# An RWKV-7 recurrence step in another order: masks split by operand, the inverse's last rows ahead of the second state, two stores issued by SP

## The chip, the cores and the metric

One core of a Trainium2 chip runs the whole program. The metric is the device time of one execution in microseconds, the median of several runs. TensorE (PE) multiplies matrices, VectorE (DVE), ScalarE (ACT) and GpSimd (POOL) work elementwise, SyncE (SP) issues DMAs; ACT can issue DMAs too.

## The reference

A decoder trunk of two layers over 1024 tokens of width 1024, with RMS norms and residual adds. The even layer (a chunked gMLP beside dilated attention) is not touched. The odd layer is RWKV-7 time mixing: projections r, k, v, a gate, a data-dependent decay, and a recurrence over time for each of 16 heads with a 64 x 64 state:

```
sa    = state @ (-kk_t)
state = state * w_t + outer(sa, kk_t * a_t) + outer(v_t, k_t)
y_t   = state @ r_t
...
y = (groupnorm(y) + bonus) * silu(g) ;  x = x + y @ w_o
```

## The kernel before

All arithmetic is in float32; a projection's operands are split into a high and a low float32r part and multiplied in three passes (`mm3`).

**The recurrence in chunks.** Time is cut into 16 chunks of 64 tokens. In a chunk the recurrence is a triangular system: U = X (W), where X is the inverse of a 64 x 64 triangular matrix per head that does not depend on the state, and W comes from the state and the chunk's keys. For chunk c, with the names of the text below:

- `al` (`alphas`): scores that give the triangular matrix M and the masked operand AK. `sM` (`store_M`) writes M to DRAM in four DMAs for a pair of chunks, `lM` (`load_M`) reads it back in another layout as Nt.
- `ip`, `ia`, `ie`, `ib`, `ic` (`inverse_p` to `inverse_c`): the inverse of a pair of chunks. POOL clears its tiles (`ip`); DVE builds diagonal blocks of 8 (`ia`, `ie`) and then block rows, eight pieces in all, of which `ibN` does the next N; `ic` stores the result to DRAM. `lX` (`load_X`) reads it back as X, and `mx`, `ma`, `mb` merge its halves of 32 with two small sets of matmuls and ACT copies between them.
- `sc` (`scores`): the scores of the outputs, copied to MY. `msk` (`masks`): POOL zeroes the upper triangles of MY and AK, two instructions for each and chunk.
- `dec` (`decayed`): POOL scales BK by the chunk's decay; `T` (`transposed`): PE transposes the scaled BK, ACT copies it to BKT.
- `U`: PE multiplies X with W (and begins the next chunk's W with AK and V), ACT copies U into UV in two halves. `st` (`state`): PE multiplies BKT with UV, DVE adds the product to the next state S. `keep`: POOL scales S by the decay ahead of that add. `W`: PE multiplies S (and the previous chunk's outputs with S). `Y` (`Yout`): PE multiplies MY with UV; `Yd` (`store_Y`): two DMAs store the outputs of a pair of chunks.
- `ld`, `uv`: SP loads A, BK and v of a later chunk. `g`: one eighth of a gate projection tile (three matmuls of 512 columns), which fills PE; every eighth such piece ends with a copy and a store issued by ACT. `gl`, `gx`: load and split of that gate's weights.

**One step** is a pair of chunks c = 2b and c + 1; in it the recurrence runs for this pair, the inverse of the next pair is finished (`ib2` and the later `ib`, `ic0`, `lX0`, merge) and the inverse of the pair after is begun (`lM0`, `ia0`, `ie0`, `ib3`). There are six steps (b = 0 to 5) between an opening part (`SCAN_START`) and a closing part (`SCAN_END`) in which the layer's output stage begins: the last pair of chunks, the output norm and the projection.

**What sets the order.** PE, DVE, ACT, POOL and SP each execute their instructions strictly in the order in which the strings `SCAN_START`, `SCAN_STEP` and `SCAN_END` name them (a manual schedule), each engine as soon as its next instruction's inputs and buffers are there. SP and ACT each have a DMA queue. A DMA also waits for the landing of the DMA that used its completion semaphore before; eight semaphores go round. The text of a step:

```
    "U0 al0 ib2 st0 al1 sM0 uv0 Y0 keep1 ib1 W1 sc0 ib1 U1 uv1 ld6 st1 sc1 ib1 ic0 dec0 Y1 lM0 W2 keep2 ip0 lX0 "
    "gx1 sc2 Yd0 T0 msk0 g2 ia0 sc3 g2 mx0 ma0 ie0 g2 dec1 T1 mb0 msk1 g3 ib3 ld7 gl2")
```

A number is an argument: for most names the chunk or pair counted from the step's own (`ops`), for `sc` half chunks, for `g` and `ib` the number of pieces. The two state adds of a step are those of `st0` and `st1`.

Of the kernel before, what the change touches and what calls it, by code (L numbers as in the profile page):

```python
# [12 lines left out]
OP = mybir.AluOpType  # L13
# [5 lines left out]
KT = D // P  # L19
# [6 lines left out]
CH = 64  # L26
# [24 lines left out]
    "q0 k0 h0 z2 h1 q1 h2 k1 h3 va0 s0 h4 u0 h5 z3 h6 z0 h7 va1 s1 u1 z1")  # L51
SCAN_START = (
# [4 lines left out]
SCAN_STEP = (  # L57
    "U0 al0 ib2 st0 al1 sM0 uv0 Y0 keep1 ib1 W1 sc0 ib1 U1 uv1 ld6 st1 sc1 ib1 ic0 dec0 Y1 lM0 W2 keep2 ip0 lX0 "
    "gx1 sc2 Yd0 T0 msk0 g2 ia0 sc3 g2 mx0 ma0 ie0 g2 dec1 T1 mb0 msk1 g3 ib3 ld7 gl2")
SCAN_END = (  # L60
# [6 lines left out]


def order(text):
    for tok in text.split():  # L70
        name = tok.rstrip("0123456789")
        yield name, int(tok[len(name):])
# [905 lines left out]
class Rwkv:  # L978
# [71 lines left out]
    def store_M(self, b2):  # L1050

        M = self.ring("M", b2, 2, None)
        for k in range(4):
            b = k % 2
            self.g.nc.scalar.dma_start(self.g.MA_d[b2][k].rearrange("c q t s -> t (c q) s"),
                                     M[32 * k:32 * k + 32, :, :, 32 * b:32 * b + 32].rearrange("p c q s -> p (c q) s"))

    def decayed(self, c):
# [13 lines left out]
                    nc.tensor.transpose(pt[:, i, :], BK[:, 4 * q + i].rearrange("p j t -> p (j t)"), g.ident)  # L1072
                nc.scalar.activation(BKT[:, 4 * q:4 * q + 4], pt, AF.Copy)

    def masks(self, c):
        nc, t = self.g.nc, self.T[c]
        for r in (slice(0, 64), slice(64, 128)):
            nc.gpsimd.affine_select(t["MY"][r], t["MY"][r], pattern=[[0, NHD], [1, CH]], compare_op=OP.is_ge, fill=0.0,
                                    base=0, channel_multiplier=-1)
            nc.gpsimd.affine_select(t["AK"][r], t["AK"][r], pattern=[[0, KT], [1, CH]], compare_op=OP.is_ge, fill=0.0,  # L1080
                                    base=-1, channel_multiplier=-1)

# [210 lines left out]

    def store_Y(self, b):
        for e in range(2):
            self.g.nc.scalar.dma_start(self.g.Y_d[b].rearrange("(c t) h d -> t c h d", c=2)[:, :, 8 * e:8 * e + 8],
                                     self.Y[64 - 64 * e:128 - 64 * e])

    def start(self, gate):
        g, nc = self.g, self.g.nc

        def zs(i):
            nc.gpsimd.memset(self.new_S(0), 0.0)

        self.pm = g.bB([P, 2, 2, 4, CH], "pm")
        ops = dict(L=gate.load, wx=gate.split, xl=gate.load_x, ld=self.load,
                   g=lambda i: [next(gate.rest, None) for _ in range(i)],
                   sc=lambda i: self.scores(i // 2, i % 2), al=self.alphas, sM=self.store_M, lM=self.load_M,  # L1310
                   ip=self.inverse_p, ia=self.inverse_a, ie=self.inverse_d, ib=lambda i: [next(self.rows, None) for _ in range(i)],
                   ic=self.inverse_c, lX=self.load_X, mx=self.merge_x, ma=self.merge_a, mb=self.merge_b,
                   dec=self.decayed, T=self.transposed, msk=self.masks,
                   uv=self.load_uv, V=lambda i: list(self.Wkeys(i)), W=self.W, keep=self.keep, zs=zs)
        for name, i in order(SCAN_START):
            ops[name](i)

    def ops(self, b, gate):
        c = 2 * b
        return dict(  # L1320
            U=lambda i: self.U(c + i), st=lambda i: self.state(c + i), keep=lambda i: self.keep(c + i),
            W=lambda i: self.W(c + i), sc=lambda i: self.scores(c + 4 + i // 2, i % 2),
            al=lambda i: self.alphas(c + 4 + i), sM=lambda i: self.store_M(b + 2 + i),
            lM=lambda i: self.load_M(b + 2 + i), ip=lambda i: self.inverse_p(b + 2 + i),
            ia=lambda i: self.inverse_a(b + 2 + i),
            ie=lambda i: self.inverse_d(b + 2 + i), ib=lambda i: [next(self.rows, None) for _ in range(i)],
            ic=lambda i: self.inverse_c(b + 1 + i), lX=lambda i: self.load_X(b + 1 + i),
            mx=lambda i: self.merge_x(b + 1 + i), ma=lambda i: self.merge_a(b + 1 + i),
            mb=lambda i: self.merge_b(b + 1 + i), dec=lambda i: self.decayed(c + 4 + i),
            T=lambda i: self.transposed(c + 4 + i), Y=lambda i: self.Yout(c + i),  # L1330
            msk=lambda i: self.masks(c + 4 + i), R=lambda i: list(self.Ystate(c + i)),
            uv=lambda i: self.load_uv(c + 2 + i), ld=lambda i: c + i < NC and self.load(c + i),
            g=lambda i: [next(gate.rest, None) for _ in range(i)],
            gl=lambda i: b + KT + i < 2 * KT and gate.load(b + KT + i),
            gx=lambda i: b + KT + i < 2 * KT and gate.split(b + KT + i),
            Yd=lambda i: self.store_Y(b + i))
# [10 lines left out]
    def end(self, gate, o):  # L1347

        g = self.g
        ops = self.ops(NB - 2, gate)  # L1350

        def store_Y(i):
            self.store_Y(NB - 2 + i)
            if i == 0:
                self.new_Y()

        self.new_Y()
        ops.update(Yd=store_Y, S=lambda i: o.setup_norm() if i else o.setup(), Sb=lambda i: o.bonus(), Lr=o.load, Ls=o.split, Fl=o.operands, Fm=o.centre, Fv=o.variance, Fy=o.scaled,
                   Ft=o.gated, Fs=o.parts, Pl=o.residual, p=o.project, Pn=o.norm, Po=o.store)
        for name, i in order(SCAN_END):  # L1360
            ops[name](i)
# [199 lines left out]
```

## Time and profile before

| | us |
|---|---|
| median of 3 runs | 1486.93 (1485.79 to 1487.78) |
| profiled execution, its own time | 1486.46 |
| its span in the trace | 1484.4 |
| PE busy | 1305.9 (88% of the span) |
| DVE busy | 913.4 (62%) |
| ACT busy | 628.8 (42%) |
| POOL busy | 544.7 (37%) |

The trace holds one execution, instruction by instruction, with times from the span's start. The busy shares are averages over the whole program; the recurrence's six steps lie between about 1080 and 1303 us, the closing part behind them.

### The profile page before, as it was taken

The page shows a single profiled execution, that of the slowest core. Times are in us where ns is not written, and L with a number is a line of the kernel's source. Part 1 is how long each engine was busy: PE and PEld are TensorE (multiplying, and loading weights), DVE is VectorE, ACT ScalarE, POOL GpSimd, SP SyncE. Part 2 cuts the span into 40 slices and gives each one's busy share as a digit, 9 for nine tenths or more (in the row PEclk, how much of TensorE's full clock was granted, in tenths as well). Part 3 has the DMA queues.
Part 4 walks back from the last instruction along what each step waited for, and adds up shares of the span by engine and source line. Part 5 has one row for each costly group of instructions (what it writes and reads, how often), then busy time and mean ns, then how long its engine had stood idle before and what let it go on. Part 6 is the DMA issues. An engine that isn't in the chain of part 4 may idle for free.

```text
span 1484.4 us, 30909 instructions
## 1 busy us (share of the span) xinstructions
PE 1305.9 (88%) x12773; PEld 1110.6 (75%) x12773; DVE 913.4 (62%) x1489; ACT 628.8 (42%) x1188; POOL 544.7 (37%) x353
## 2 busy tenths in 40 slices
PE   5899999799998999999998869998977878687877
PEld 5887788788896799978854537896766667567877
DVE  8741536663556436760698997332676776668884
ACT  4421535543554324652555554232434444354322
POOL 8750102030213512221343353023744444367751
PEclk9999999899999999999999989998988998889999
DMA  6277446240543435133187547427675565675412
GB/s 220 86 265 188 114 128 171 72 128 15 148 108 115 141 106 152 47 110 108 50 243 196 132 118 196 105 74 218 167 234 157 154 156 145 160 220 212 145 34 95
DMA packets 253276, 209.16 MB, mean 141 GB/s; under 512 B 79648, under 2 KB 215424, under 8 KB 253136
## 3 DMA queue, kind: packets, MB, share of 16 engines
q1 hardware_dynamic: 230336, 191.98, 44.4%
q10 hardware_dynamic: 22800, 15.21, 3.7%
q8 instruction: 100, 1.64, 0.5%
q14 instruction: 40, 0.33, 0.1%
HBM read 135.71 MB, written 71.43 MB: 140 GB/s over the span
## 4 chain that ended last, share of the span: by engine, by line
PE 51%; DVE 17%; DMA 12%; ACT 7%; issue 6%; POOL 4%; SPq 2%; ACTq 1%; DVEq 0%; POOLq 0%
PE pj L153 33%; PE pj L943 3%; PE pt L572 2%; PE pj L1473 2%; PE pj L711 2%; DMA X<-XT 1%; DMA XT<-xm 1%; DMA w<-in_rw_a_dram 1%; DMA BK<-BK_d 1%; PE ch L1271 1%; PE op L580 1%; ACT wh L105 1%; PE sp L559 1%; PE sp L562 1%; ACT UV L1250 1%
## 5 line engine op out<-in xcount | busy, mean ns | idle before, releaser
L106 POOL TENSOR_TENSOR wl<-wraw,wh 128x1024 fp32r<-128x1024 f32 x38 | 95.6, 2518 | 174.2 <-ACT wh L105 161.5
L153 PE MATMUL pj<-hh,wh 128*128 128x512 f32 x320 | 127.3, 398 | 0.0
L153 PE MATMUL pj<-hh,wl 128*128 128x512 f32 x320 | 126.7, 396 | 0.0
L153 PE MATMUL pj<-hl,wh 128*128 128x512 f32 x320 | 126.6, 396 | 0.0
L106 DVE TENSOR_TENSOR wl<-wraw,wh 128x1024 fp32r<-128x1024 f32 x46 | 71.7, 1564 | 84.7 <-ACT wh L105 44.0
L105 ACT ACTIVATE wh<-wraw 128x1024 fp32r<-128x1024 f32 x84 | 88.2, 1057 | 66.0 <-DMA wraw<-in_w_in_even_dram 23.3
L153 PE MATMUL pj<-xl,wh 128*128 128x512 f32 x256 | 104.2, 408 | 2.5 <-DVE xl L740 2.5
L153 PE MATMUL pj<-xh,wh 128*128 128x512 f32 x256 | 103.8, 408 | 2.5 <-ACT ks L789 2.5
L153 PE MATMUL pj<-xh,wl 128*128 128x512 f32 x256 | 103.6, 405 | 0.2 <-POOL wl L106 0.2
L566 DVE CUSTOM_DVE_ANT_0 sc<-sp,tb 128x128 f32<-128x128 f32 (+3 forms) x64 | 48.2, 754 | 58.0 <-PE sp L562 49.6
L1473 PE MATMUL pj<-wh,yl 128*128 128x256 f32 x256 | 74.1, 289 | 6.4 <-POOL yl L106 6.4
L1473 PE MATMUL pj<-wh,yh 128*128 128x256 f32 x256 | 74.8, 292 | 5.2 <-DVE x L1477 5.2
L153 PE MATMUL pj<-wh,hh 128*128 128x256 f32 x256 | 74.7, 295 | 2.9 <-ACT hh L265 2.6
L737 DVE SCALAR_TENSOR_TENSOR xm<-hT,pr,xm 128x512 f32<-128x512 f32 x56 | 49.0, 917 | 44.1 <-ACT xm L736 43.7
L153 PE MATMUL pj<-wh,hl 128*128 128x256 f32 x256 | 74.8, 293 | 1.2 <-DVE hl L266 1.2
L153 PE MATMUL pj<-wh,yl 128*128 128x256 f32 x256 | 73.8, 288 | 1.9 <-POOL yl L624 1.9
L153 PE MATMUL pj<-wl,hh 128*128 128x256 f32 x256 | 74.3, 291 | 0.0
L1473 PE MATMUL pj<-wl,yh 128*128 128x256 f32 x256 | 73.8, 288 | 0.0
L153 PE MATMUL pj<-wh,yh 128*128 128x256 f32 x256 | 73.3, 286 | 0.5 <-ACT yh L623 0.5
L153 PE MATMUL pj<-wl,yh 128*128 128x256 f32 x256 | 72.9, 285 | 0.0
L153 PE MATMUL pj<-wh,xh 128*128 128x256 f32 x256 | 72.2, 282 | 0.1
L153 PE MATMUL pj<-wl,xh 128*128 128x256 f32 x256 | 72.2, 282 | 0.0
(320 smaller groups left out, 4063.2 us busy)
## 6 DMA issues: line engine op xcount, KB each, us to landing
wraw<-in_w_in_even_dram SPq DMA_DIRECT2D x28, 512.0 KB
tb<-tb SPq DMA_DIRECT2D x16, 512.0 KB
A_d<-AR SPq DMA_DIRECT2D x16, 512.0 KB
wraw<-in_rw_wg_dram SPq DMA_DIRECT2D x16, 512.0 KB
A<-A_d SPq DMA_DIRECT2D x16, 512.0 KB
BK<-BK_d SPq DMA_DIRECT2D x16, 512.0 KB
xt<-in_x_dram SPq DMA_DIRECT2D x8, 512.0 KB
dv<-vt SPq DMA_DIRECT2D x16, 256.0 KB
```

The source lines that it names most:

```text
L105: nc.scalar.activation(hi, raw, AF.Copy)
L106: sub.tensor_tensor(lo, raw, hi.bitcast(F32), OP.subtract)
L153: nc.tensor.matmul(ps, a(k), b(k), start=(n == 0), stop=(n == 3 * KT - 1))
L559: nc.tensor.matmul(sp[:, c0:c1], qs[:, b * P:(b + 1) * P], kh[:, c0:c1], start=True, stop=False)
L562: nc.tensor.matmul(sp[:, c0:c1], qs[:, b * P:(b + 1) * P], kl[:, c0:c1], start=False, stop=True)
L566: nc.vector.tensor_tensor_reduce(sc[:, :n], sp[:, :n], tb[:, off:off + n], 1.0, BIG, OP.add, OP.min, mn)
L572: nc.tensor.transpose(pt[:, j - j0, :], sc[:, j * P:(j + 1) * P], g.ident)
L580: nc.tensor.matmul(op[:, s0:QW], vt[:, j, :], pth[j // 4][:, j % 4, s0:QW], start=(j == 0), stop=False)
L711: nc.tensor.matmul(ps, x[:, 2 * kk + i, :], y[:, i, o:o + 512], start=(n == 0), stop=(n == 47))
L737: nc.vector.scalar_tensor_tensor(t, hT[kk, f][:, j, 0:512], g.pr[:, i, k:k + 1], t, op0=OP.mult, op1=OP.add)
L943: nc.tensor.matmul(ps, u[:, k], v[:, k % 2], start=(k == 0 and i == 0), stop=(k == KT - 1 and i == 2))
L1473: nc.tensor.matmul(ps[:, i, :], u[:, k], v[:, k % 4], start=(k == 0 and j == 0), stop=(k == KT - 1 and j == 2))
```

## The change

`masks` becomes two functions: `mask_AK`, called in a step for the chunks whose scores were just made (c+4, c+5), ahead of the second `W`, and `mask_MY`, called a step later than before (c+2, c+3), ahead of the second state. Of the inverse's rows the last three pieces are done together ahead of the second `U` (DVE) where one of them stood behind the second state; `ic0` follows ahead of `st1`. Scores `sc1` and two gate pieces move up, `mb0` and `T1` change places. The stores of M and of the outputs are issued by SP in place of ACT: M behind the first load of v, ahead of `ld6`; the outputs behind `lX0`, ahead of `ld7`. The first load of v of a step moves to the end of the step before. The opening and the closing part follow; the closing part now holds two `mask_MY` (four POOL instructions) that a step held before.

```diff
 SCAN_START = (
-    "ld3 L6 g4 msk0 ia0 L5 g2 al2 wx5 g2 sc4 T1 ld4 g3 al3 sM1 ie0 sc5 dec2 g3 wx6 ib8 sc6 g2 sc7 dec3 uv1 T2 zs0 "
-    "g3 ic0 g4 wx7 msk1 ip1 lM1 lX0 keep0 g4 T3 g5 L8 mx0 xl0 V0 ma0 g2 wx8 xl1 ia1 msk2 g2 xl2 mb0 ie1 W0 ld5 "
-    "msk3 g2 xl3 ib3")
+    "ld3 L6 g4 mA0 mY0 ia0 L5 g2 al2 wx5 g2 sc4 T1 ld4 g3 al3 sM1 ie0 sc5 dec2 g3 wx6 ib8 sc6 g2 sc7 dec3 uv1 T2 "
+    "zs0 g3 ic0 g4 wx7 mA1 mY1 ip1 lM1 lX0 keep0 g4 T3 g5 L8 mx0 xl0 V0 uv2 ma0 g2 wx8 xl1 ia1 mA2 g2 xl2 mb0 ie1 "
+    "W0 ld5 mA3 g2 xl3 ib3")
 SCAN_STEP = (
-    "U0 al0 ib2 st0 al1 sM0 uv0 Y0 keep1 ib1 W1 sc0 ib1 U1 uv1 ld6 st1 sc1 ib1 ic0 dec0 Y1 lM0 W2 keep2 ip0 lX0 "
-    "gx1 sc2 Yd0 T0 msk0 g2 ia0 sc3 g2 mx0 ma0 ie0 g2 dec1 T1 mb0 msk1 g3 ib3 ld7 gl2")
+    "U0 al0 ib2 st0 al1 Y0 uv1 keep1 mA0 mA1 W1 sM0 sc0 ib3 ld6 U1 sc1 g1 mY0 mY1 ic0 st1 dec0 lM0 Y1 g1 W2 keep2 "
+    "ip0 lX0 gx1 uv2 sc2 Yd0 T0 g1 sc3 ia0 ld7 mx0 ma0 dec1 ie0 g2 mb0 g2 T1 g2 ib3 gl2")
 SCAN_END = (
-    "Lr1 S0 Fl0 uv0 U0 g1 Fm0 ib2 Lr5 Lr2 st0 Y0 keep1 g1 ib1 W1 Lr6 uv1 ib1 Lr7 Ls5 U1 ib1 ic0 Ls2 gx1 lX0 Ls7 "
-    "st1 Sb0 Y1 Ls1 Ls6 Fv0 W2 keep2 Fl1 mx0 g4 ma0 g2 mb0 Yd0 Lr0 g2 Pl1 U2 Fm1 Fy0 st2 Fv1 Lr4 Lr3 Fy1 Y2 W3 "
...
+    "Lr1 S0 Fl0 U0 ib2 g1 Fm0 Lr5 Lr2 st0 Y0 keep1 mY0 mY1 g1 W1 ib3 Lr6 uv1 Lr7 Ls5 U1 ic0 Ls2 gx1 lX0 Ls7 st1 "
+    "Sb0 Y1 Ls1 Ls6 Fv0 W2 keep2 Fl1 mx0 g4 ma0 g2 mb0 Yd0 Lr0 g2 Pl1 U2 Fm1 Fy0 st2 Fv1 Lr4 Lr3 Fy1 Y2 W3 Ls0 "
...
@@ -1052,7 +1052,7 @@
         M = self.ring("M", b2, 2, None)
         for k in range(4):
             b = k % 2
-            self.g.nc.scalar.dma_start(self.g.MA_d[b2][k].rearrange("c q t s -> t (c q) s"),
+            self.g.nc.sync.dma_start(self.g.MA_d[b2][k].rearrange("c q t s -> t (c q) s"),
                                      M[32 * k:32 * k + 32, :, :, 32 * b:32 * b + 32].rearrange("p c q s -> p (c q) s"))
...
-    def masks(self, c):
+    def mask_AK(self, c):
+        nc, t = self.g.nc, self.T[c]
+        for r in (slice(0, 64), slice(64, 128)):
+            nc.gpsimd.affine_select(t["AK"][r], t["AK"][r], pattern=[[0, KT], [1, CH]], compare_op=OP.is_ge, fill=0.0,
+                                    base=-1, channel_multiplier=-1)
+
+    def mask_MY(self, c):
         nc, t = self.g.nc, self.T[c]
         for r in (slice(0, 64), slice(64, 128)):
             nc.gpsimd.affine_select(t["MY"][r], t["MY"][r], pattern=[[0, NHD], [1, CH]], compare_op=OP.is_ge, fill=0.0,
                                     base=0, channel_multiplier=-1)
-            nc.gpsimd.affine_select(t["AK"][r], t["AK"][r], pattern=[[0, KT], [1, CH]], compare_op=OP.is_ge, fill=0.0,
-                                    base=-1, channel_multiplier=-1)
...
     def store_Y(self, b):
         for e in range(2):
-            self.g.nc.scalar.dma_start(self.g.Y_d[b].rearrange("(c t) h d -> t c h d", c=2)[:, :, 8 * e:8 * e + 8],
+            self.g.nc.sync.dma_start(self.g.Y_d[b].rearrange("(c t) h d -> t c h d", c=2)[:, :, 8 * e:8 * e + 8],
                                      self.Y[64 - 64 * e:128 - 64 * e])
...
-                   dec=self.decayed, T=self.transposed, msk=self.masks,
+                   dec=self.decayed, T=self.transposed, mA=self.mask_AK, mY=self.mask_MY,
...
-            msk=lambda i: self.masks(c + 4 + i), R=lambda i: list(self.Ystate(c + i)),
+            mA=lambda i: self.mask_AK(c + 4 + i), mY=lambda i: self.mask_MY(c + 2 + i), R=lambda i: list(self.Ystate(c + i)),
```

## Rows read from the trace of the kernel before

**Rows 1.** Busy us by engine, six steps; then granted clock, DMA share, GB/s.
```profile
1080.00:1303.00 223.00, 171.06 (x4859) 144.90 (x4858) 158.05 (x251) 88.61 (x155) 93.02 (x92) 0.88 0.63 169
```

**Rows 2.** Waits of PE, six steps: total us, times, longest.
```profile
PE pt L1193 <- DMA X<-XT: 16.3, 9, 3.1
PE ch L1271 <- ACT UV L1250: 8.4, 11, 1.2
```

**Rows 3.** Timeline, DVE: first adds of steps 1, 6, closing part.
```profile
1091.36 0.68 DVE L1273 TENSOR_TENSOR S<-ch,S 128x512 f32<-128x512 f32 x1
...
1267.49 0.68 DVE L1273 TENSOR_TENSOR S<-ch,S 128x512 f32<-128x512 f32 x1
...
1307.12 0.69 DVE L1273 TENSOR_TENSOR S<-ch,S 128x512 f32<-128x512 f32 x1 [3.53 <-PE ch L1271]
```

**Rows 4.** Timeline, DVE, fourth step: start, us, instruction, idle before.
```profile
1198.68 0.68 DVE L1273 TENSOR_TENSOR S<-ch,S 128x512 f32<-128x512 f32 x1
...
1205.01 0.69 DVE L1273 TENSOR_TENSOR S<-ch,S 128x512 f32<-128x512 f32 x1 [2.02 <-PE ch L1271]
1205.62 0.95 DVE L1158 TENSOR_TENSOR tm<-DN,R 128x768 f32<-128x768 f32 x1
1206.60 0.95 DVE L1160 TENSOR_REDUCE xm<-tm 128x96 f32<-128x768 f32 x1
...
1214.10 0.92 DVE L1117 TENSOR_TENSOR DN<-Nt,rn 128x256 f32<-128x256 f32 x1 [2.74 <-DMA Nt<-MA]
...
1232.13 0.68 DVE L1273 TENSOR_TENSOR S<-ch,S 128x512 f32<-128x512 f32 x1
```

**Rows 5.** Timeline, SP's DMA issues, fourth step.
```profile
1201.09 1.11 SPq L1003 DMA_DIRECT2D BK<-BK_d  x1
1207.59 1.27 SPq L1167 DMA_DIRECT2D XT<-xm  x2
```

**Rows 6.** Timeline, ACT and PE, fourth step.
```profile
1196.29 1.97 ACTq L1055 DMA_DIRECT2D MA<-M  x4
...
1203.74 1.15 PE L1271 MATMUL ch<-UV,BKT 128*64 128x64 f32 x32 [1.23 <-ACT UV L1250]
...
1217.46 0.31 PE L1193 MATMUL pt<-X,M 32*32 32x32 f32 x8 [1.67 <-DMA X<-XT]
...
1227.97 1.20 ACT L1250 ACTIVATE UV<-ch 64x512 f32<-64x512 f32 x2 [2.16 <-PE ch L1246]
```

**Rows 7.** Waits of DVE, six steps.
```profile
DVE S L1273 <- PE ch L1271: 22.6, 6, 6.3
```

**Rows 8.** Groups of POOL's instructions, six steps (busy us, mean ns).
```profile
L1078 POOL TENSOR_SCALAR_AFFINE_SELECT MY<-MY 64x1024 f32<-64x1024 f32 x25 | 29.0, 1158 | 2.1 <-ACT MY L1031 1.4
...
L1080 POOL TENSOR_SCALAR_AFFINE_SELECT AK<-AK 64x512 f32<-64x512 f32 x25 | 18.3, 730 | 0.0
```

**Rows 9.** One group of DVE's instructions by shape, six steps.
```profile
L1127 DVE TENSOR_TENSOR tm<-DN 128x36 f32<-128x36 f32 x6 | 6.8, 1137 | 0.2
```

**Rows 10.** Timeline, DVE, sixth step, where POOL was idle beside it.
```profile
1286.99 0.20 DVE L1127 TENSOR_TENSOR tm<-DN 128x36 f32<-128x36 f32 x1
```

**Rows 11.** Timeline, POOL, fourth step.
```profile
1199.51 1.74 POOL L1262 TENSOR_TENSOR S<-S,EC 128x512 f32<-128x512 f32 x1 [10.84 <-DVE S L1273]
...
1208.30 1.06 POOL L1262 TENSOR_TENSOR S<-S,EC 128x512 f32<-128x512 f32 x1
1211.97 0.55 POOL L1102 MEMSET xm<- 128x544 f32 x1 [2.61 <-DMA XT<-xm]
...
1216.72 1.91 POOL L1062 TENSOR_TENSOR BK<-BK,EC 128x1024 f32<-128x1024 f32 x1
```

**Rows 12.** Timeline, ACT, end of the sixth step.
```profile
1296.12 1.20 ACT L1196 ACTIVATE rt<-pt 32x512 f32<-32x512 f32 x2 [8.01 <-DMA BK<-Y]
```

**Rows 13.** Timeline, POOL and DVE, closing part.
```profile
1312.14 10.49 POOL L106 TENSOR_TENSOR wl<-wraw,wh 128x1024 fp32r<-128x1024 f32 x4 [2.44 <-ACT wh L105]
...
1315.21 2.88 DVE L106 TENSOR_TENSOR wl<-wraw,wh 128x1024 fp32r<-128x1024 f32 x1 [1.77 <-ACT wh L105]
```

8 rows, old and new, of the table SCAN_END are left out of this document.

## The prediction

> **What bounds the kernel now.** First the busy time of the stretch that the change touches: six recurrence steps, from 1080 to 1303 us, in which TensorE is busy for 171.06 of 223 us at a mean granted clock of 0.88 [rows 1]. So a sixth of the tensor work's time there is waiting, and TensorE is not at its limit. Then who it waits for: 16.3 us go to the merge's first matmul, which waits for the DMA that brings back the inverse X, and 8.4 us to the state's matmul, which waits for ScalarE's two copies of U [rows 2]. Third, the distance between steps. The clearest mark is DVE's first state add of a step (call its end E): the first of the six is at 1091.36 and the sixth at 1267.49, so five steps take 176.1 us, 35.2 each; the next one, in the closing part, follows 39.6 later [rows 3].
>
> Last, one step read in order of time, the fourth. E is 1199.36. DVE does four more pieces of the inverse, then idles 2.02 us for TensorE before the second state add at 1205.01; only then come the last two rows, which end at 1207.55 [rows 4]. At 1207.59 SP issues the store of the inverse, and behind it in the same queue the load of the next Nt [rows 5]. Nt has landed when DVE starts the next inverse at 1214.10, and from there DVE works without a pause up to the next first add at 1232.13 [rows 4], 33.4 us after the last. TensorE stands still for it. This is a closed loop: E, rows, store, Nt, next inverse, next E. A second loop runs through X: the merge starts at 1217.46, when X has landed, and U is copied out at 1227.97 [rows 6]. In the other steps the hole before the second add is larger (six holes, 22.6 us, at most 6.3 [rows 7]), and the second loop decides.
>
> **The change, part by part.**
>
> *The last rows before the second add.* Two instructions, 1.93 us from 1205.62 to 1207.55 [rows 4], move from behind the add into the hole before it. The smallest hole is 2.02 us, so the add hardly moves. The store of the inverse goes out as soon as the six pieces are done: 3.63 us for the first four (1199.36 to the hole's start at 1202.99) and 1.93 for the last two, E+5.6 instead of E+8.2 here, and up to 7 us earlier where the hole was long.
>
> *The masks split.* Eight instructions on POOL, four of 1.16 us (MY) and four of 0.73 us (AK) [rows 8], lie today beside DVE's next inverse. There DVE's small two-operand instructions are held up: the worst, of 36 elements, takes 1.14 us on average and 0.20 with POOL idle [rows 9, 10], a loss of 0.94. It is one of eight such forms; the other seven, compared in the same way, lose from 0 to 0.6 each and 2.6 together, so 3.5 of the chain's 18.0 us. Moved ahead, the masks lie beside the three two-operand pieces that follow E. Each of these can lose from nothing to the rest of one mask, 0.6 on average if all collide: 0 to 1.8 in all, I take 0.9. The store is then at E+6.5. Nobody needs the masks soon (AK in the next step's second U, MY in the next step's outputs).
>
> *What the masks are put in front of.* On POOL they now precede the scaling of BK, the scaling of S and the preparation of the next inverse, which DVE needs. The line from E: scaling S 1.9 (E to 1201.25), masks 7.6, BK 1.91, S 1.06, preparation 1.0 (1211.97 to 1212.99) [rows 8, 11], sum 13.5. If three two-operand DVE instructions there (two pieces and the weight split) hold POOL for their length, each like the 0.95 of the last rows' first one [rows 4], 16.4. I take 15.5, nearer the upper end, because the scaling of S shows such a hold-up now: 1.74 us beside DVE, 1.06 without. The other input, Nt, lands 6.5 us after the store, at E+13.0, so POOL is what is late next. The transposes on TensorE wait for BK until about E+14, but TensorE only reaches the merge after that and X is not there before E+16.4 (store E+6.5, 4.4 to its landing at 1211.97, 5.5 to 1217.46), so this wait is covered.
>
> *The period that follows.* Next inverse from E+15.5; the chain is 18.0 less 3.5, plus the second BK scaling (1.91 [rows 11]), which still falls into it and can cost 0 to 1.9: I take 0.5, so 15.0; the add 0.7. Together 31.2. The loop through X: E+16.4, then 10.5 to the copy of U and 0.8 for one more gate piece behind the merge, then copies 1.2, state 1.15 [rows 6], add 0.8: 30.9. The larger is 31.2, so five steps take 156.0 in place of 176.1: **20.1 less**. Bounds of the period: below 29.5 (of the 5.5 us in which X comes back, the four issues are about 2.0, like those of M [rows 6]; the other 3.5 may shrink by 1.4, an estimate, once the output store no longer runs beside them), above 33.5 (POOL 16.4, the full 1.9).
>
> *Gate pieces and scores ahead of the second state.* They fill 1.2 us of the wait for U, eleven such waits in rows 2. That work is only moved, and X decides the step's length: nothing by itself.
>
> *Stores issued by SP.* ScalarE loses six issues a step (the four M stores took 1.97 us [rows 6]) while it waits for TensorE: nothing. On SP the M stores come after the first U load, ahead of the loads of A and BK and of the inverse's store; SP stands idle there until 1207.59, so nothing in the normal case; its other case is a rival below. The output store is put behind the X loads, and the loads behind it have 10 us to spare.
>
> *Into the closing part.* In the last step ScalarE is held 8.01 us by a gate store that waits for a load far down the queue [rows 12], which makes that interval 39.6. The queue starts filling some 4 us earlier: 4 less (0 to 8). In the closing part POOL gets four MY masks, 4.6 us, ahead of four weight splits that run without pause for 10.5 us, and DVE's own split already takes 2.88 us beside them [rows 13]; 2.4 us of idle time before them take up half. So 2 more (0 to 4). The opening part gives back at most 1 us, since its first step waits for a load; I take nothing.
>
> **Sum.** 20.1 + 4 - 2 = 22.1 less. The profiled execution took 1486.46 us (span 1484.4), which gives 1464.4; the median of the runs is 0.5 above it. Predicted: 1465.
>
> **Rivals.**
> *Half the gain.* SP now issues the M stores and 1 MB of A and BK close ahead of the inverse's store. Today that load is out at 1201.09, 6.5 us before [rows 5], so their meeting is not shown. If the store's small packets wait for these bytes, X and Nt land 2 to 3 us later, and the period closes near 33.5: 8.6 + 4 - 2 less, 1476. The Trainium skill (DMA: Bandwidth & Descriptors, Queues, rings and completion order) says that each DMA engine takes a ring's descriptors in order, and that SP has one ring on each; by that rule the store waits whenever SP is late. No row of before shows it.
> *No gain.* The next inverse starts not at E+15.5 but at E+19.5, for whatever mixture of the two; then the period is the old 35.2 and the rest cancels: 1486.
> *Slower, through POOL.* Its line in front of the next inverse is the one place where the change adds work to a chain. It decides from E+19.5 on; at E+21.5 the period is 37.2, ten more for five steps and two in the closing part: 1498. For it: POOL's instructions lengthen beside DVE. Against it: the rows allow 16.4. The Trainium skill (SBUF, Who interferes with whom) has the two engines lock each other out for a whole instruction when DVE reads two operands from SBUF; by that rule the line cannot pass the sum of both, and the trace agrees (scaling S 1.74 beside 1.06).
> *The rows move but the add pays.* If the last rows overran the hole, the second add would be late by up to 1.8 us; two TensorE pieces cover it. Counted in the first rival.
>
> **Chances.** The likeliest 0.58 (own range 1457 to 1473), half the gain 0.20, still more (period 29.5, 1456) 0.04, no change 0.07, slower 0.11. A measurement of this kernel can tell about 0.2%, 3 us, from no change. Faster 0.82, same 0.07, slower 0.11. The range leaves out the last two cases and little below: 1453 to 1480.
>
> **What would show it.** Right: no DVE work between the second add and the weight split; the inverse's store near E+6.5; first adds 31 us apart; the wait for X below half of 16.3; 36-element instructions near 0.3 us. Wrong: next inverse later than E+17 with Nt long landed (POOL), X more than 10 us after its store (queue), or a longer closing part.

## The result, and the profile after

The changed kernel takes 1478.93 us (median of 17 runs, 1468.73 to 1484.7) against 1487.78 for the kernel before (1484.98 to 1495.47): ratio 0.9929, 95% interval 0.9911 to 0.9947. That is inside the predicted range, but 8.9 us of gain where 22 were predicted. The profiled execution took 1480.0 us (span 1478.1), 6.5 less than that of before.

Where the 6.3 us between the two spans come from is read off DVE's first state adds, those of the first, second and sixth step and the closing part (they answer to [rows 3]). E is the end of a step's first state add, as in the prediction:

```profile
1096.76 0.68 DVE L1277 TENSOR_TENSOR S<-ch,S 128x512 f32<-128x512 f32 x1
...
1131.01 0.69 DVE L1277 TENSOR_TENSOR S<-ch,S 128x512 f32<-128x512 f32 x1 [2.99 <-PE ch L1275]
...
1263.90 0.69 DVE L1277 TENSOR_TENSOR S<-ch,S 128x512 f32<-128x512 f32 x1 [2.09 <-PE ch L1275]
...
1296.41 0.69 DVE L1277 TENSOR_TENSOR S<-ch,S 128x512 f32<-128x512 f32 x1 [1.33 <-PE ch L1275]
```

| | before | predicted | after | after, second profile |
|---|---|---|---|---|
| first add of the first step | 1091.36 | 1091.4 | 1096.76 | 1091.18 |
| five intervals | 176.1 | 156.0 | 167.1 | 167.1 |
| each | 35.2 | 31.2 | 33.4 | 33.4 |
| last interval | 39.6 | 35.6 | 32.5 | 36.1 |
| closing part, from that add to the end | 177.3 | 179.3 | 181.7 | 181.8 |

The first line is not the change: in a second execution (first experiment) it is at 1091.18, and the 5.6 us lie ahead of the recurrence (the first load of BK is issued at 1009.3 in the one and 1003.8 in the other). The five intervals agree: 9.0 us gained where 20.1 were forecast.

One step of the changed kernel, the fourth, on SP's queue (issues; answers to [rows 5]) and on DVE:

```profile
1199.27 1.13 SPq L1013 DMA_DIRECT2D UV<-v_d  x2
1200.49 2.24 SPq L1055 DMA_DIRECT2D MA<-M  x4
1202.83 1.36 SPq L1001 DMA_DIRECT2D A<-A_d  x1
1204.29 0.38 SPq L1003 DMA_DIRECT2D BK<-BK_d  x1
1204.76 1.26 SPq L1171 DMA_DIRECT2D XT<-xm  x2
1206.19 4.30 SPq L1099 DMA_DIRECT2D Nt<-MA  x2
1212.00 2.92 SPq L1179 DMA_DIRECT2D X<-XT  x4
```

```profile
1197.30 0.68 DVE L1277 TENSOR_TENSOR S<-ch,S 128x512 f32<-128x512 f32 x1
...
1203.14 0.95 DVE L1164 TENSOR_REDUCE xm<-tm 128x96 f32<-128x768 f32 x1
...
1207.95 0.69 DVE L1277 TENSOR_TENSOR S<-ch,S 128x512 f32<-128x512 f32 x1 [3.85 <-PE ch L1275]
...
1214.35 1.23 DVE L106 TENSOR_TENSOR wl<-wraw,wh 128x1024 fp32r<-128x1024 f32 x1 [5.71 <-ACT wh L105]
1215.49 0.42 DVE L1121 TENSOR_TENSOR DN<-Nt,rn 128x256 f32<-128x256 f32 x1
```

The rows are done at 1204.09 (E+6.1, E = 1197.98), ahead of the second add, as planned. SP, which stood idle at this point before, comes from the M stores and the two loads without a pause and issues the store at 1204.76. It stays in the issue of N's load for 4.30 us, and the load of X, which waits for the store's landing, goes out 7.24 us after the store. The next inverse (1215.49) starts right behind DVE's split of a gate's weights, which waits 5.71 us for ACT's half of that split; in this step it is not N that holds the inverse. In the other four of the first five steps DVE waits 1.6 to 1.8 us for N.

Waits of PE and DVE in 1080 to 1303 us (total, times, longest; they answer to [rows 2, 7]), and groups by shape (answers to [rows 8, 9]):

```profile
PE pt L1197 <- DMA X<-XT: 10.4, 7, 3.3
PE ch L1275 <- ACT UV L1254: 2.1, 5, 0.7
...
DVE S L1277 <- PE ch L1275: 25.5, 10, 3.9
DVE DN L1121 <- DMA Nt<-MA: 6.8, 4, 1.8
```

```profile
L1131 DVE TENSOR_TENSOR tm<-DN 128x36 f32<-128x36 f32 x7 | 1.4, 197 | 0.2
...
L1084 POOL TENSOR_SCALAR_AFFINE_SELECT MY<-MY 64x1024 f32<-64x1024 f32 x27 | 31.8, 1177 | 1.4
L1078 POOL TENSOR_SCALAR_AFFINE_SELECT AK<-AK 64x512 f32<-64x512 f32 x24 | 21.9, 913 | 0.9
```

The masks are off DVE's chain (0.197 us for the 36-element instruction, 1.137 before), but PE still waits 10.4 us for X (the prediction's sign of being right was less than half of 16.3), and DVE 6.8 us for N: the loops through DRAM did not close as early as forecast.

The end of the sixth step on ACT, and the closing part on POOL and DVE (they answer to [rows 12, 13]):

```profile
1283.56 0.35 ACTq L950 DMA_DIRECT2D sg_d<-XT  x1
1283.95 0.60 ACT L1031 ACTIVATE MY<-pm 128x512 f32<-128x512 f32 x1 [2.97 <-DMA Y<-Y]
1284.44 1.18 ACT L1200 ACTIVATE rt<-pt 32x512 f32<-32x512 f32 x2
```

```profile
1298.94 5.74 POOL L1084 TENSOR_SCALAR_AFFINE_SELECT MY<-MY 64x1024 f32<-64x1024 f32 x4
1304.77 10.34 POOL L106 TENSOR_TENSOR wl<-wraw,wh 128x1024 fp32r<-128x1024 f32 x4
...
1312.80 3.40 DVE L106 TENSOR_TENSOR wl<-wraw,wh 128x1024 fp32r<-128x1024 f32 x1 [3.98 <-POOL wl L106]
```

The gate's store waits 2.97 us on ACT where it waited 8.01. In the closing part the masks run without a pause into the splits, and DVE waits 3.98 us for one of those.

### The profile page after: what moved, and what is told of

Read it like the earlier page. It is cut to its first block, busy times and chain, and to the rows that moved or that the text cites. A ratio compares the mean times of both kernels' runs of the same rounds, so it can differ in the third digit from the quotient of the medians.

```text
span 1478.1 us, 30910 instructions
## 1 busy us (share of the span) xinstructions
PE 1308.3 (89%) x12773; PEld 1108.9 (75%) x12773; DVE 897.8 (61%) x1489; ACT 627.8 (42%) x1188; POOL 548.4 (37%) x353
## 4 chain that ended last, share of the span: by engine, by line
PE 53%; DVE 17%; DMA 9%; issue 8%; ACT 6%; POOL 4%; SPq 2%; ACTq 0%; DVEq 0%; POOLq 0%
PE pj L153 33%; PE pj L943 4%; PE pt L572 2%; PE pj L1477 2%; DMA kl<-dk 1%; DMA BK<-BK_d 1%; DMA w<-in_rw_a_dram 1%; DMA XT<-xm 1%; PE sp L562 1%; PE sp L559 1%; PE op L580 1%; DMA X<-XT 1%; ACT wh L105 1%; PE py L1285 1%; DVE xm L737 1%
```

## The experiments

All are edits of the changed kernel, with ratios to the kernel before on the same chip. The medians come from several chips, so ratios are compared. The changed kernel itself gave 0.9929 and 0.9884, further apart than their 95% intervals allow. So a difference of less than 0.005 shows nothing by itself between rows that were not run together (together are the second to the fifth row, the sixth to the ninth and the last four). For each step with five intervals the table has the means of the inverse's store, counted from E; of SP's first load of X behind the store (in nearly all of them it goes out when the store has landed); of the next inverse's start behind the store; and the interval, all from one profiled execution. "Ratio" has its 95% interval.

| kernel | store, E+ | X behind store | inverse behind store | interval | last | closing | median us | ratio |
|---|---|---|---|---|---|---|---|---|
| changed, first profile | 7.7 | 6.8 | 9.3 | 33.4 | 32.5 | 181.7 | 1478.93 | 0.9929 (0.9911 to 0.9947) |
| changed, again | 7.8 | 6.7 | 8.8 | 33.4 | 36.1 | 181.8 | 1474.73 | 0.9884 (0.9859 to 0.9909) |
| M on ACT | 6.1 | 6.0 | 10.6 | 32.4 | 37.7 | 181.6 | 1473.70 | 0.9877 (0.9849 to 0.9905) |
| loads late | 6.3 | 4.7 | 8.5 | 30.9 | 34.2 | 181.5 | 1467.19 | 0.9837 (0.9815 to 0.9859) |
| both | 6.2 | 5.1 | 9.1 | 31.3 | 40.0 | 181.1 | 1468.19 | 0.9847 (0.9825 to 0.9869) |
| half the loads late | 6.8 | 5.8 | 8.4 | 33.2 | 33.5 | 181.2 | 1466.78 | 0.9866 (0.9835 to 0.9897) |
| loads on ACT | 6.2 | 6.8 | 10.0 | 32.0 | 33.5 | 181.3 | 1472.49 | 0.9896 (0.9873 to 0.9919) |
| loads late, gate stores on SP | 6.3 | 4.4 | 8.4 | 30.6 | 30.4 | 182.1 | 1457.97 | 0.9791 (0.9767 to 0.9814) |
| loads late, closing masks in front | 6.8 | 4.7 | 8.4 | 30.9 | 34.7 | 179.1 | 1463.41 | 0.9832 (0.9808 to 0.9856) |
| masks at the old place | 7.0 | 7.1 | 9.5 | 35.1 | 34.4 | 178.7 | 1479.65 | 0.9912 (0.9895 to 0.9929) |
| rows at the old place | 11.8 | 4.0 | 7.0 | 35.0 | 37.3 | 181.4 | 1489.43 | 0.9987 (0.9967 to 1.0006) |
| all three edits | 6.3 | 4.7 | 8.8 | 30.8 | 34.4 | 178.6 | 1457.00 | 0.9766 (0.9748 to 0.9784) |
| all three, M on ACT | 6.2 | 4.6 | 8.4 | 31.0 | 34.4 | 178.7 | 1459.38 | 0.9790 (0.9774 to 0.9806) |

The same intervals cut at three instructions of DVE show where the waits lie (means of five steps, us; with the first add's 0.7 the three parts make the interval). Beside them stand the clock that TensorE was granted over the five intervals, as a share of 2.4 GHz, and how long PE was busy in them:

| kernel | E to the second state add | from that to the next inverse (of it waiting for N) | from that to the next first add (of it that add waiting for PE) | granted clock | PE busy, five intervals |
|---|---|---|---|---|---|
| before | 7.5 | 9.5 (2.2) | 17.5 (0) | 0.90 | 139.9 |
| changed, first profile | 8.9 | 8.1 (1.4) | 15.8 (1.4) | 0.89 | 140.1 |
| M on ACT | 10.0 | 6.7 (0) | 15.0 (0) | 0.91 | 135.6 |
| loads late | 8.6 | 6.2 (0) | 15.4 (0) | 0.98 | 130.1 |
| half the loads late | 8.6 | 6.6 (0.2) | 17.3 (2.1) | 0.86 | 146.2 |
| loads on ACT | 9.4 | 6.8 (0.4) | 15.2 (0.3) | 0.94 | 133.0 |
| masks at the old place | 8.2 | 8.2 (1.1) | 17.9 (0.4) | 0.87 | 144.7 |
| rows at the old place | 8.7 | 10.1 (3.4) | 15.5 (1.7) | 0.86 | 143.5 |

The clock belongs to the argument. In the first interval of the changed kernel PE waits 2.29 us for X, up to 1114.86, and for most of the next 10 us it is granted the lower of its two levels, 1.2 GHz; the next first add then waits 2.99 us for PE. With the loads late the same stretch of the first step runs at 2.4 GHz throughout. Rows of the changed kernel, then one of the kernel with the loads late (busy us and counts of PE, PEld, DVE, ACT and POOL, then granted clock, DMA share, GB/s):

```profile
1111.00:1115.00 4.00, 1.53 (x37) 0.91 (x36) 1.78 (x3) 2.29 (x5) 3.17 (x4) 1.00 0.90 178
1115.00:1125.00 10.00, 9.84 (x143) 7.92 (x142) 9.30 (x25) 2.35 (x4) 0.00 (x0) 0.52 0.79 234
```

```profile
1113.00:1126.00 13.00, 10.79 (x307) 9.00 (x302) 12.20 (x28) 6.32 (x11) 0.88 (x1) 1.00 0.85 279
```

In the changed kernel's two profiles six of the ten intervals have a mean granted clock of 0.90 or less, and each ends with a wait of the first add for PE, 1.6 to 3.0 us; the other four (0.92 to 0.95) end with none. No run changes the clock alone, so what the clock costs beside the waits themselves is not separated.

**The changed kernel again.**

> The changed kernel again, as the reference of this group of runs and to see how far its executions differ ahead of the recurrence. Time near 1479. If the 5.9 us by which its first profile was late at the end of the projections is variation between executions, a second profile puts the first state add elsewhere than at 1096.8; if it belongs to the change, again at 1096 to 1097. The five intervals of the state adds are 33 to 33.8 each in either case.

As expected: first add at 1091.18, five intervals 167.1. The single ones scatter from 30.8 to 37.4, so a mean over five is the least that can be compared.

**M stores on ACT.**

```diff
-            self.g.nc.sync.dma_start(self.g.MA_d[b2][k].rearrange("c q t s -> t (c q) s"),
+            self.g.nc.scalar.dma_start(self.g.MA_d[b2][k].rearrange("c q t s -> t (c q) s"),
```

> The changed kernel with the stores of M issued by ACT again. Theory A (the store of the inverse and its landing set the interval, because SP issues the M stores and 1 MB of loads just ahead of it): the M stores' 2.2 to 3 us on SP go, the inverse's store issues at 6.1 to 6.8 behind the state add instead of 6.8 to 8.4, N lands 1 to 1.5 us earlier, the interval falls from 33.4 to 32 to 32.5, in sum 5 to 7 us faster. Rival B (POOL's masks, memset and decay set the start of the next inverse): POOL is not earlier, under 2 us. Rival C (ACT's issue of four stores, which the change took off ACT, costs the copies behind it as much): ACT's copy of the next W or U is later by up to 2 us and the sum is 0 or a loss.

The store goes out at E+6.1, as soon as the rows are done, so SP's turn with M was what held it back by 1.5 us. But little comes of it (32.4, and about the same ratio). SP now waits for the M stores to land before it loads N (first line, SP's waits over the six steps), yet DVE waits for N in none of the five steps. What is late is the second state add, at E+10.0 in the mean where the changed kernel has 8.9: ACT's four issues stand ahead of its copies of MY, and PE waits 12.8 us for those copies (second line), 0.6 in the changed kernel.

```profile
SPq L1099 <- DMA MA<-M: 14.3, 12, 3.1
SPq L1171 <- DVE xm L1164: 11.4, 5, 3.1
```

```profile
PE pm L1030 <- ACT MY L1031: 12.8, 11, 2.7
```

In time that is rival B's "under 2 us", but by ACT and not by POOL, and theory A is only half borne out. ACT's copies are what it cost, as rival C had it (the copies of MY, by up to 2.7 us), and the kernel's time is 1.0 us less on the same chip, inside the noise. The opening became 3 us shorter: from the first BK load to the first add it takes 84.3 us, and 87.3 to 88.8 in the eight profiles with M on SP and the gate's stores on ACT. In the changed kernel's opening PE waits 8.1 us for the first X, which it does not do here (nor in the kernel before).

**Loads late.** `ld6` moves behind the loads of X:

```diff
-    "... W1 sM0 sc0 ib3 ld6 U1 sc1 ..."
+    "... W1 sM0 sc0 ib3 U1 sc1 ... ip0 lX0 gx1 uv2 ld6 sc2 ..."
```

> The changed kernel with the 1 MB of A and BK loads (ld6) issued behind the four loads of X instead of ahead of the inverse's store; the M stores stay on SP. Theory A: the store issues at 6.1 to 6.7 behind the state add, its landing and N's are no longer behind 1 MB on the ring, N lands 6.5 to 7.5 behind the store instead of 9.0, so the interval falls to 31.2 to 32 and the sum is 7 to 11 us faster. Rival B (POOL): N lands earlier but the inverse starts at the end of POOL's line, about 15 behind the state add, the interval stays above 32.5 and the gain under 4. Rival D (the X loop on PE): N earlier, but the next state add waits longer for PE and the interval stays.

The fourth step on SP, beside that of the changed kernel above, and PE's wait for X in the six steps:

```profile
1191.40 3.17 SPq L1055 DMA_DIRECT2D MA<-M  x4
1194.76 1.27 SPq L1171 DMA_DIRECT2D XT<-xm  x2
1196.34 1.17 SPq L1099 DMA_DIRECT2D Nt<-MA  x2
1199.87 2.84 SPq L1179 DMA_DIRECT2D X<-XT  x4
```

```profile
PE pt L1197 <- DMA X<-XT: 1.5, 2, 0.8
```

X goes out 5.11 us behind the store instead of 7.24, PE's wait for it falls from 10.4 to 1.5 us, and the interval is 30.9: close to the forecast's 31.2, with everything else of the change as it is. Rivals B and D fall. But the path that now closes the interval is not one of the forecast's. In none of the five intervals does DVE wait for N, or a first add for PE, the granted clock is 0.98 instead of 0.89, and the inverse starts 6.1 to 6.5 us behind the second state add; here it is the fourth step on DVE:

```profile
1198.31 0.69 DVE L1277 TENSOR_TENSOR S<-ch,S 128x512 f32<-128x512 f32 x1 [3.62 <-PE ch L1275]
...
1203.28 1.23 DVE L106 TENSOR_TENSOR wl<-wraw,wh 128x1024 fp32r<-128x1024 f32 x1 [4.27 <-ACT wh L105]
1204.42 0.42 DVE L1121 TENSOR_TENSOR DN<-Nt,rn 128x256 f32<-128x256 f32 x1
...
1219.45 0.68 DVE L1277 TENSOR_TENSOR S<-ch,S 128x512 f32<-128x512 f32 x1
```

DVE waits 4.27 us for ACT's half of the gate's weight split (`gx`), which stands in ACT's order behind the copies of the next W, and these wait for the second state. That path is read from the trace; no run moves `gx`.

**Both.**

> Both edits: the M stores on ACT and ld6 behind the loads of X. Theory A: the sum of the two up to the forecast's interval of 31.2, 10 to 12 us faster than the changed kernel, 1466 to 1469. Rival B or D: no more than the better one of the two alone, under 4.

No sum: 31.3 in the steps, and the last interval 40.0, where the gate's store on ACT waits 7.2 us for a landing again and the second add comes only at E+13.4. M on ACT gives nothing once the loads are out of the way; PE waits 9.9 us for ACT's copies of MY here too.

**Half the loads late.** Only BK's 512 KB move, A's stay ahead of the store.

```diff
-    "... ib3 ld6 U1 ... uv2 sc2 ..."
+    "... ib3 la6 U1 ... uv2 lb6 sc2 ..."
```

> The changed kernel with only the half of ld6 that is BK (512 KB) moved behind the loads of X; the half that is A (512 KB) stays ahead of the inverse's store. Theory A (the bytes ahead of the store set its landing): half of what moving both gave, an interval of about 32.2 (the changed kernel 33.4, with both moved 30.9), N lands about 8 to 8.5 behind the store, ratio to the kernel before about 0.986 to 0.987. Rival E (what counts is that SP is busy issuing the loads, two issues of 0.6 to 0.9 us): also half of the issue delay, but the landing behind the store stays at 9 or more once the store is out. Rival F (a threshold, any load ahead costs it all, or none): the interval is 33.4 or 30.9.

X goes out 5.8 us behind the store: halfway between 4.7 with nothing ahead of it and 6.8 with 1 MB, and the ratio lies where it was expected, in a range too narrow to tell much. Rival F falls for the landing. The interval is undecided: the profiled execution shows 33.2 and was the slowest of six (1477.15; the others 1462.4 to 1473.9). What closes it there is the loop through X: DVE hardly waits for N (0.9 us in all), but in four of the five intervals the first add waits 2.1 to 3.3 us for PE, PE waits 8.5 us for X, and its granted clock is 0.86.

**Loads on ACT.** Same place in the order, other queue.

```diff
-            ld=lambda i: c + i < NC and self.load(c + i),
+            ld=lambda i: c + i < NC and self.load(c + i, self.g.nc.scalar if i == 6 else None),
```

> The changed kernel with ld6 at its old place in the order but issued by ACT, so its 1 MB lies on ACT's queue and SP's order is M stores, inverse's store, loads of N and X. Theory G (order on SP's queue: what is ahead on the same queue must go first): the full gain as with ld6 behind X, interval 31 to 31.5, ratio about 0.984. Theory H (the two queues share the same engines and the bytes cost wherever they are issued): N still lands 8.5 to 9.5 behind its store, the interval is 32.4 to 33.4 and the ratio 0.987 to 0.990. Rival E (SP's issue time alone): store at 6.8 and interval 32.4. ACT pays two issues, about 1.2 us, in a place where its copies wait for PE.

ACT's and SP's issues in one step:

```profile
1162.27 0.33 ACTq L1002 DMA_DIRECT2D A<-A_d  x1
...
1164.38 0.33 ACTq L1004 DMA_DIRECT2D BK<-BK_d  x1
```

```profile
1164.00 1.27 SPq L1172 DMA_DIRECT2D XT<-xm  x2
1165.44 2.76 SPq L1100 DMA_DIRECT2D Nt<-MA  x2
1170.31 1.90 SPq L1180 DMA_DIRECT2D X<-XT  x4
```

The store goes out at E+6.2, as in the fastest kernels, and still lands as late as with the loads on SP (6.8). So for the landing neither the place in SP's queue (theory G falls) nor SP's issue time is the cause: the bytes in flight are, on whichever queue. The Trainium skill (DMA: Bandwidth & Descriptors, Queues, rings and completion order) says this too: the semaphore's increment lands only behind every earlier write of that DMA engine, across its queues. The trace agrees, 6.8 on either queue against 4.7.

For the interval this run decides less. It is 32.0, below theory H's range, 0.4 from rival E's 32.4, and 1.1 above the kernel with the loads late. DVE waits for N only 1.9 us in all, and PE waits longer for ACT's copies of U, which now stand behind the loads that ACT issues (2.1 us in the changed kernel, 2.0 with the loads late):

```profile
PE ch L1276 <- ACT UV L1255: 7.4, 8, 2.7
```

How much of the 1.1 us is the landing, how much ACT and how much the clock (0.94 and 0.98) is not separated.

**Gate stores on SP**, with the loads late.

```diff
-        g.nc.scalar.dma_start(g.sg_d[n % KT, :, f * 512:(f + 1) * 512], t)
+        g.nc.sync.dma_start(g.sg_d[n % KT, :, f * 512:(f + 1) * 512], t)
```

> The kernel with ld6 behind the loads of X, and with the gates' stores (sg) issued by SP instead of ACT. Theory: in the last step ACT holds the copies of the merge back while its sg store waits for the landing of an earlier transfer (6.25 us in the kernel with ld6 moved, 8.0 in the kernel before, 3.0 in the changed one); without it the last interval falls from 34.2 to 29 to 31, and the rest stays, 1462 to 1465. Rival: the merge then waits for X or for SP's queue instead, and the last interval stays at 33 to 34; or SP, waiting for the gate's copy, delays the loads behind it and the steps grow by 0.5 to 1 each (a loss of up to 4).

The merge's copies on ACT follow PE with no DMA between them, and the last interval falls to 30.38:

```profile
1258.06 1.21 ACT L1200 ACTIVATE rt<-pt 32x512 f32<-32x512 f32 x2 [1.16 <-PE pt L1197]
```

```profile
1240.08 0.68 DVE L1277 TENSOR_TENSOR S<-ch,S 128x512 f32<-128x512 f32 x1
...
1270.46 0.69 DVE L1277 TENSOR_TENSOR S<-ch,S 128x512 f32<-128x512 f32 x1
```

So the last interval follows in the main how long that store waits on ACT: 8.0 before (39.6), 3.0 and 6.5 in the two executions of the changed kernel (32.5 and 36.1), 6.3 with the loads late (34.2). It is not all: M on ACT has 8.4 and 37.7, both edits 7.2 and 40.0. The opening is shorter as well, 84.2 us against 88.8 with the loads late, about as much of the gain as the last interval.

**Closing masks in front**, with the loads late.

```diff
-    "Lr1 S0 Fl0 U0 ib2 g1 Fm0 Lr5 Lr2 st0 Y0 keep1 mY0 mY1 g1 W1 ..."
+    "mY0 mY1 Lr1 S0 Fl0 U0 ib2 g1 Fm0 Lr5 Lr2 st0 Y0 keep1 g1 W1 ..."
```

> The kernel with ld6 behind the loads of X, and with the four MY masks of the closing part put at its front, where POOL is idle for 18 us, instead of ahead of the first W. Theory: the 4.4 us by which the closing part grew in the changed kernel comes from these 4.7 us of masks ahead of POOL's splits, so it goes back by 3 to 4.5: from the closing part's first state add to the end 177 to 178.5 instead of 181.5. Rival: the closing part is set by something else (DVE, PE's output projection), and it stays at 181 to 182.

The closing part goes back to 179.1, 2.4 of the 4.4 us; the kernel's time can't be told from that without the edit.

**Masks at the old place.** `mY` and `mA` of a chunk together behind `T0` and behind `mb0`.

```diff
-    "... keep1 mA0 mA1 W1 ... g1 mY0 mY1 ic0 ... Yd0 T0 g1 sc3 ... g2 mb0 g2 T1 ..."
+    "... keep1 W1 ... g1 ic0 ... Yd0 T0 mY0 mA0 g1 sc3 ... g2 mb0 mY1 mA1 g2 T1 ..."
```

> The changed kernel with its masks where the kernel before had them: AK and MY of one chunk together behind T0 and behind the merge; rows, stores and all else as changed. By the prediction the split of the masks is what puts the DVE chain from the next inverse's start to its last row at 15.0 us, since 36- and 64-element steps of 0.2 us no longer wait 1 to 3 us each for a mask on POOL. So the chain grows by the 3 to 4 us that it had before, the interval from 33.4 to 35 to 37, ratio 0.995 to 1.003, if the chain sets the end. Rival (the changed kernel's interval is set by X and PE, and the chain has the 1.9 to 3.0 us of slack that the first state adds wait for PE): only 1 to 2 us a step, ratio 0.990 to 0.995.

The hold-ups return to DVE's chain (0.87 us for the 36-element instruction); from the inverse's start to the next first add it takes 17.9 us, 15.8 in the changed kernel. DVE's adds wait less for PE (8.2 us, 25.5 in the changed kernel), but by the trace 11.9 us, four times, for POOL's scaling of BK, which with no masks ahead of it stands beside the second add:

```profile
L1131 DVE TENSOR_TENSOR tm<-DN 128x64 f32<-128x64 f32 x6 | 7.3, 1209 | 0.2
L1131 DVE TENSOR_TENSOR tm<-DN 128x36 f32<-128x36 f32 x6 | 5.2, 871 | 0.2
```

The interval grows by 1.7, at the lower end of what the first theory expected. The ratio is the rival's, but it lies between the changed kernel's own two; the closing part, without masks, is 3.0 shorter.

**Rows at the old place.**

```diff
-    "... mA1 W1 sM0 sc0 ib3 ld6 U1 sc1 g1 mY0 mY1 ic0 st1 dec0 ..."
+    "... mA1 ib1 W1 sM0 sc0 ib1 ld6 U1 sc1 g1 mY0 mY1 st1 ib1 ic0 dec0 ..."
```

> The changed kernel with the last rows of the inverse spread between W1, U1 and the second state add again, and the store behind that add; masks and stores as changed. The rows' end then lies about 10 to 11 behind the first state add instead of 6.1. Theory A (the store cannot issue before 7.5 to 8.4 anyway, SP being busy with the M stores and ld6): the move is worth only the rest, the interval grows by 2 to 3, ratio 0.994 to 1.000. Rival (by the prediction's own path the full move of 4 to 5 counts): interval 37.5 to 38.5, ratio 1.003 to 1.008. Rival (X has slack, the rows' place matters little): under 1 each, ratio 0.988 to 0.992.

PE's wait for X is 24.5 us, the interval 35.0, the last 37.3, the whole gain is gone. Theory A's ratio holds, its 2 to 3 for the interval is 1.6. The store goes out 4.1 us later (E+11.8) but has landed only 1.3 later, as it lands in 4.0 us instead of 6.8 where the loads were issued longer before it. So of the 4.1 us by which the change brings the rows forward, 1.3 are left at the landing. With either part undone the steps are back near the kernel before's 35.2 (35.1 and 35.0): in the changed kernel rows and masks pay only together. With the masks back it is DVE's chain that grows, with the rows back the wait for N (3.4 us a step, 1.4 in the changed kernel).

**All three edits.**

> The changed kernel with the three edits that gave something: ld6 behind the loads of X, the sg stores on SP, the four closing MY masks at the front of the closing part. If the gains lie in different places they add: 1458 with the first two, less 2.4 in the closing part, 1455 to 1456, ratio 0.977 to 0.978. If the masks at the front collide there with the now earlier end of the last step, no more than the first two, 1458.

1457.0 us, 0.9766: the lowest ratio, though it can't be told from the 0.9791 without the masks in front, and not by adding. The last interval is 34.4 instead of 30.4, the closing part 178.6 instead of 182.1. Two of the masks in front come ahead of the tiles that POOL prepares for the last inverse (the copy is at 1258.87; in the kernel without this edit, another execution, at 1254.97). DVE's chain starts 0.8 us later behind E, waits 0.8 for that copy, and its first instructions take longer beside the other two masks (1.03 us for the 4-element one, 0.17 without this edit):

```profile
1253.74 2.35 POOL L1084 TENSOR_SCALAR_AFFINE_SELECT MY<-MY 64x1024 f32<-64x1024 f32 x2
1256.17 1.90 POOL L1266 TENSOR_TENSOR S<-S,EC 128x512 f32<-128x512 f32 x1
...
1258.87 0.24 POOL L1110 COPY DN<-rn 128x32 f32<-128x32 f32 x1
```

**All three with M on ACT.**

> The same with the M stores on ACT. For: in the two kernels with M on ACT the first state add came 3 us earlier behind the first loads (84.3 and 84.9 instead of 87.4 to 88.8). Against: with the sg stores off ACT that opening already fell to 84.2, and ACT pays 4 issues a step. Theory: no gain in the opening now, 0 to 1 a step lost, 1455 to 1460; if M on SP still delays the opening's loads, 1452 to 1454.

Nothing gained (0.9790): the opening is as short without it once the gate stores are on SP.

## Why the prediction was half wrong, step by step

- **What bounds the steps: right, but not complete.** A loop through E, rows, store, N and the next inverse, and one through X. Both are seen in the changed kernel: over the five intervals the inverse waits 6.8 us for N and the first adds 7.0 us for PE. Moving the loads alone took the interval from 33.4 to 30.9. What then closes it in the trace is a third path, which the forecast does not have: second state add, ACT's and DVE's halves of the gate's weight split, next inverse.
- **Last rows ahead of the second add: right.** Done at E+6.1 (forecast: store at E+6.5); no DVE work stands between the second add and the weight split. The add itself did move, from E+7.5 in the mean before to 8.9, and 8.6 with the loads late. With the rows at the old place it is at 8.7 too, so the rows are not the cause. The scores and the gate piece ahead of it, which the forecast put at nothing, were not tested alone.
- **Masks split: right.** The 36-element instructions take 0.20 us; the chain, forecast at 15.0, takes 15.4 with the loads late. POOL, forecast to be ready at E+15.5, is so at E+14.5 to 15.5 there, and DVE waits for it once, 0.8 us; in the changed kernel nowhere. The rival "slower, through POOL" fell.
- **Stores issued by SP: this step failed**, at "so nothing in the normal case", and with it "the other input, Nt, lands 6.5 us after the store, at E+13.0". The rows moved ahead to the very moment at which SP issues the M stores and 1 MB of loads. The store went out at E+7.65 in the mean, 1.3 later than in the kernel with the loads late (6.32), and landed 2.1 later (6.8 and 4.7); the inverse started near E+16.9 instead of E+14.8. That makes the period 33.4, almost the 33.5 of the rival "half the gain", which was given 0.20. Its mechanism was right in the bytes; the order in SP's ring, which it cites, is not needed for it, as the landing is the same 6.8 with the loads on ACT's queue. That the interval is 30.9 where only the loads are moved shows that this term was worth the 11.1 us missing in the steps (moving them gave 12.7). How the interval divides between SP's issue time and the landing stays open, since both runs that would part them (M on ACT, loads on ACT) hold up ACT's copies. In the rows part of the cost goes with TensorE's clock, for which the forecast has no term: 0.89 over the five intervals, 0.98 with the loads late, with PE busy 140.1 and 130.1 us.
- **The forecast's 31.2 beside that 30.9 is partly luck.** It has the inverse start at E+15.5, behind POOL; with the loads late it starts at E+14.8, behind the weight split, behind an add that is itself later than before, and the chain is 0.4 longer than forecast. The lower bound of 29.5 does not follow from its own working either: it shortens the loop through X and leaves the other at 31.2.
- **Last interval: mechanism right, size scattered.** Forecast 4 less; 7.1 and 3.6 in two executions, in the main by the wait of one store on ACT.
- **Closing part: mechanism right, size short.** Forecast +2, measured +4.4 and +4.5. Masks in front bring 2.4 back, masks in the steps 3.0. What is left, 1.4, stays open.
- **Opening: forecast nothing, and nothing in the second execution**, but two things cancel there that the forecast didn't have: M on SP costs about 3 us in the wait for the first X (taking it off gives them back); what in the change gains as much is not shown. That the first execution was 5.4 late there is no part of the change; what makes executions differ ahead of the recurrence was not tried.

In sum, for the profiled execution: 22.1 less the 11.1 of the steps, plus 3.1 in the last interval, less 2.4 in the closing part and 5.4 in the opening, is 6.3. The medians, 8.9 and 16.1 below the kernel before on their chips, scatter by as much as these last terms.

## What to carry to other kernels

When a piece of work is moved earlier, look at what else the queue and the DMA engines are doing at its new moment, not at its old one: SP's idle time in the profile before was idle time at the wrong place. A short round trip through DRAM on a critical loop wants the large prefetches issued behind it, whatever queue they are on. And a DMA issued by a compute engine holds up the copies behind it there, for its issue and at times for another transfer's landing (PE's 12.8 us behind the M stores on ACT); on SP it holds up only other DMAs, so look at which of them is in a hurry. A wait of PE can cost more than its length where the granted clock falls behind it. When one loop has been shortened, read anew which wait closes the period: here it was a path that no sum had.

## What was not expected of the hardware

- The landing of the inverse's store grew evenly with the bytes of A and BK ahead of it: 4.7 us with none, 5.8 with 512 KB, 6.8 with 1 MB, and 6.8 with that 1 MB on the other queue (means of five steps of one execution; the five single ones of a kernel lie 1.3 to 2.7 apart).
- One store of 256 KB on ACT waited 3.0 to 8.4 us ahead of its issue for the landing of a transfer issued by SP, and moved the end of a step by 3.8 us (last interval 34.2 and 30.4).
- The same kernel's executions scatter by 16 us (1468.73 to 1484.7), twice what the change gained; in the kernel with the loads late, of which there are only four, by 4.5 (1463.31 to 1467.85). Of the changed kernel's 17 executions the three shortest were granted a clock of 0.948 to 0.955 over the whole span, the five longest 0.940 to 0.946.
